# A decoder trunk in split float32: two of three products joined in one 512-column matmul

## The chip, the cores and the metric

The kernel runs on one core of a Trainium2 chip. The metric is the device time of the core in microseconds (us), from runs of the whole program. The engines are TensorE (PE; its weight loads are shown apart as PEld), VectorE (DVE), ScalarE (ACT), GpSimd (POOL) and SyncE (SP), which issues the DMAs. Weights come from HBM; SBUF is the on-chip memory with 128 partitions; PSUM takes the results of TensorE in eight banks, each 128 partitions by 512 float32 values.

## The reference

The input is x with 256 tokens of 1024 values. The program is two layers. Each is wrapped by two half-step SwiGLU FFNs, so there are four FFNs, called a, b, c and d here. Between a and b stands a chunked gMLP (u, v, a spatial mixing of v), between c and d a stick-breaking attention, whose shared keys and values are computed between b and c.

```python
def swiglu(h, w_in, w_out):              # w_in 1024 x 5632, w_out 2816 x 1024
    gate, up = jnp.split(h @ w_in, 2, axis=-1)
    return (jax.nn.silu(gate) * up) @ w_out

x = x + 0.5 * swiglu(rms_norm(x, g), w_in, w_out)     # four of these

z = jax.nn.gelu(h @ a_w_in)              # gMLP, a_w_in 1024 x 4096
u, v = jnp.split(z, 2, axis=-1)
x = x + (u * (W_s @ layer_norm(v) + b)) @ a_w_out
```

All values are float32.

## The kernel before

**Products.** The weights are streamed as pieces of 128 x 1024 in the order of use: a DMA into `raw` (7 buffers), a ScalarE cast to the high part `whi` (L81, 9 buffers), a VectorE subtraction to the low part `wlo` (L83, 9 buffers). x is split in the same way into `xnh` and `xnl`. A product of full precision is three matmuls that add up in PSUM (`mm3`, L148 to L150): low weights by high x, high weights by low x, high weights by high x, each over 256 tokens, that is 256 columns.

**An FFN.** Its 2816 features are 11 blocks of 256. `ffn_in(j)` makes block j of gate and up: two matrices, 8 chunks of 128 along the contraction, 2 halves of 128 features, so 32 triples. Gate and up have one PSUM bank each, the two halves side by side. Then VectorE multiplies each bank by `rb`, the 1/rms of each token (L449 gate, L451 up), ScalarE takes silu of gate (L450), VectorE multiplies the two (L452), and the result is split into `hh` (ScalarE, L153) and `hl` (VectorE, L154). The output block `out(j)`, 16 triples, multiplies these by two pieces of the second matrix into the four `y` banks. The order is in(0), in(1), then out(j) and in(j+2) by turns; at the end the rest of out(9) and out(10) goes block by block of x (`close`), and each x block is scaled, split again and squared at once. In FFN d the output products stand the other way round, with 512 columns (`yo`), and transposes of x (`xb`, L809) lie behind in(1).

**PSUM.** Two pools of four banks each, taken in rotation: `gbank` for input blocks and everything that is used briefly, `ybank` for the residual stream. A bank is taken again as soon as the last reader of its old contents is done.

**Other users of gbank in FFN a.** Behind out(3) and out(4) the spatial weights are transposed (`pws`, read by one VectorE copy each), behind out(5) and out(6) `spatial_bias` makes a row sum in one bank (`prs`, L516), which eight VectorE instructions read (L519).

**u.** `u_in` makes 256 features of u in one bank by 16 triples, eight times; one multiplication by `rb` (L585) and a gelu follow.

**Order.** Every engine runs its queue in order. A recording layer orders the instructions of each engine by priorities and dependencies, so the place of the casts of later weight pieces between an FFN's own instructions is not that of the program text. Each cast of a piece waits until the piece nine places earlier in the stream has had its last product.

Of the kernel before, what the change touches and what calls it, by code (L numbers as in the profile page):

```python
# [28 lines left out]
WARM = 6, 10  # L29
# The attention's order of issue, by blocks of two heads: q (four heads' queries), z (scores), p  # L30
# (weights), t (weights transposed), v (values), o (products into the residual stream, in the
# banks that y sets up).
ATT_STEPS = (
# [5 lines left out]
class Weights:  # L39
    """The weight matrices as a stream of [128, 1024] pieces in the order of use. Each is loaded  # L40
    once and split exactly into two float32r parts, w = hi + lo, some pieces ahead of its use."""

    def __init__(self, tc, raw_pool, hi_pool, lo_pool):
        self.nc = tc.nc
        self.keep_order = tc.keep_in_program_order
        self.strict = False
        self.behind = 0  # so many pieces keep their place
        self.piece = UNIT
        self.pools = raw_pool, hi_pool, lo_pool
        self.sources = []  # L50
        self.raw = {}
        self.parts = {}
        self.loaded = 0
        self.split = 0
# [5 lines left out]
    def order(self, ins):  # L60
        """Keeps an instruction behind those traced ahead of it, where the order matters."""
        return self.keep_order(ins) if self.strict else ins
# [37 lines left out]
def trunk(  # L100
# [44 lines left out]
    def mm3(o, a, b, first, last):  # L145
        """o (+)= a.T @ b for a, b each given as two float32r parts."""
        (ah, al), (bh, bl) = a, b
        nc.tensor.matmul(o, al, bh, start=first, stop=False, skip_group_check=True)  # L148
        nc.tensor.matmul(o, ah, bl, start=False, stop=False, skip_group_check=True)  # L149
        nc.tensor.matmul(o, ah, bh, start=False, stop=last, skip_group_check=True)  # L150
# [4 lines left out]

    # The gMLP's blocks of 256 features: the u products, the mixing behind them, the products into
    # the residual stream behind that.
    U_STEPS = [("in", 0), ("in", 1)]
# [5 lines left out]

# [1 line left out]
    W = Weights(tc, rawp, hip, lop)  # L166
# [7 lines left out]
    def plan_in_out(n, ins, w_out):  # L174
        """Pairs of blocks: columns of the first matrix, then, one pair later, the rows that they
        meet in the second."""
        steps = {}
        for j in range(n + 1):
            if j < n:
                steps["in", j] = [[W.add(cols(w, c0 + 256 * j, kh)) for w, c0 in ins] for kh in range(2)]  # L180
            if j:
                steps["out", j - 1] = [W.add(rows(w_out, 256 * (j - 1) + P * m)) for m in range(2)]
        return steps
# [19 lines left out]

# [1 line left out]
    xin = {}  # L205
# [37 lines left out]
    def warm_up(n):  # L243
        """Products of nothing, that wake the tensor engine's clock while the first loads run."""
        bank = gbank("warm")
        for _ in range(n):
            W.order(nc.tensor.matmul(bank[:, :P], ones, ones, start=True, stop=True))
# [11 lines left out]

# [1 line left out]
    xT = act.tile([P, KC, T], F32, name="xT")  # L261
    xnh = act.tile([P, KC, T], F32R, name="xnh")
    xnl = act.tile([P, KC, T], F32R, name="xnl")
    acc = act.tile([P, T], F32, name="acc")
# [4 lines left out]
    def prepare(d, gains, sq=True):  # L269
        """The parts of x*g of chunk d for the next products, and its share of the mean square."""  # L270
        for (name, i), h, l in gains:
            g = gain(name, i * KC + d)
            W.order(nc.scalar.activation(h[:, d, :], xT[:, d, :], AF.Copy, scale=g))
            W.order(
                nc.vector.scalar_tensor_tensor(
                    l[:, d, :], xT[:, d, :], g, h[:, d, :].bitcast(F32), ALU.mult, ALU.subtract
                )
            )
        if sq:
            square(d)  # L280
# [12 lines left out]
    def newton(o, root, v, w):  # L293
        """o = v**-0.5 from an estimate of v**0.5, with a step of Newton's; w is scratch."""
        nc.vector.reciprocal(o, root)
# [4 lines left out]
    class Rms:  # L300
        """1/rms of each token: first as a column per 128 tokens (rT), then along the free axis on
        all partitions (rb)."""

# [23 lines left out]

# [1 line left out]
    def load_x(hf):  # L329
        """Half of x into the residual stream, its parts and its squares."""  # L330
        for d in range(hf * 4, hf * 4 + 4):
# [32 lines left out]
    def bc2(ap):  # L364
        """[128, n] -> [128, 2, n], the same twice."""
        return ap.unsqueeze(1).broadcast_to([P, 2, ap.shape[1]])

    def pair(ap):
        return ap.rearrange("p (m t) -> p m t", m=2)

# [1 line left out]
    class Residual:  # L372
        """y.T = sum over chunks of W[chunk].T @ h[chunk], in four banks."""

# [12 lines left out]
    def close(y, tail, head, scale, gains):  # L387
        """The last chunks block by block, so that each block of x is ready early; head blocks of
        the first of them go ahead."""
        w, h = tail[0]  # L390
# [10 lines left out]
    def project(outs, ids, xs, mid={}, by_bank=False):  # L401
        """outs += W.T x for blocks of 256 features: [features, tokens] of two halves each. mid:
        what else is done behind a number of groups."""
        groups = []
# [3 lines left out]
        for n, group in enumerate(groups):  # L408
# [12 lines left out]
            if n + 1 in mid:  # L421
                mid[n + 1]()

    def project_rows(o, ids, xs, mid={}):
        """x.T W for a block of 256 features: [tokens, features] of two halves."""
        for kh in range(2):
# [16 lines left out]
    def ffn_in(tag, j, ids, mid={}, by_bank=False):  # L443
        """silu(gate) * up of 256 features, in two parts."""
        banks = [gbank(f"g{tag}_{j}"), gbank(f"u{tag}_{j}")]
        project(banks, ids, XN, mid, by_bank)
        gs = scratch(f"gs{tag}_{j}")
        us = scratch(f"us{tag}_{j}")
        nc.vector.tensor_mul(pair(gs), pair(banks[0]), bc2(rb))  # L449
        nc.scalar.activation(gs, gs, AF.Silu)  # L450
        nc.vector.tensor_mul(pair(us), pair(banks[1]), bc2(rb))  # L451
        nc.vector.tensor_mul(us, us, gs)  # L452
# [8 lines left out]
    def ffn(tag, plan, gains, mid={}, by_bank=False, extra={}):  # L461
        """extra: what else is done ahead of a block's products into the residual stream."""
        hs = {0: ffn_in(tag, 0, plan["in", 0], mid, by_bank), 1: ffn_in(tag, 1, plan["in", 1])}
# [13 lines left out]

    # ======== layer 0: gMLP ========
    sgu = ExitStack()
# [16 lines left out]
    def spatial_weights(hf):  # L496
        """The causal W_s, transposed, and what the LayerNorm's shift and b_s add behind it:
        b_c * (row sum of W_s)[t] + b_s[t]."""
        gg = slice(hf * 4, hf * 4 + 4)
# [44 lines left out]

    # v, tokens on partitions; its LayerNorm without gain and shift, which come behind W_s.
    vsb = sg.tile([P, 2, DA], F32, tag="vsb", name="vsb")
# [34 lines left out]
    def u_in(j):  # L581
        bank = gbank(f"uu{j}")
        project([bank], [[i] for i in plan_u["in", j]], XN)
        u = sg.tile([P, 512], F32, tag="u", name=f"usb{j}", bufs=4)
        nc.vector.tensor_mul(pair(u), pair(bank), bc2(rb))  # L585
        nc.scalar.activation(u, u, AF.Gelu_apprx_tanh)
        return u
# [47 lines left out]

    # ======== shared K and V, and layer 1: stick-breaking attention ========
    att = ExitStack()
# [10 lines left out]

    # k, transposed; the row half of each head is its own, the other half is zero.
    XK = (xkh, xkl)  # L650
# [7 lines left out]
    for r in range(2):  # L658
# [3 lines left out]
        for t in kz:  # L662
            nc.gpsimd.dma_start(t[oo, r::2, 1 - r, :].bitcast(F32), t[rr, r::2, r, :].bitcast(F32))
    # v, tokens on partitions, each head twice.
    vf = scratch("vf")
# [25 lines left out]
    def weights_of(b, q):  # L691
        """A of heads 2b and 2b+1: sigmoid(z) times the product of sigmoid(-z) over the keys
        between; [queries, heads, keys] for each block of queries."""
        kv = b // 2
# [102 lines left out]

    # ======== the last FFN, its output with tokens on partitions, and the final norm ========
    fin = ctx.enter_context(tc.tile_pool(name="fin", bufs=1))
# [102 lines left out]
```

## Time and profile before

| | us |
|---|---|
| median of 3 runs | 1019.38 (1019.08 to 1020.25) |
| profiled execution, its span | 1016.9 |
| busy in the span: TensorE | 998.7 (98%) |
| weight loads | 979.4 (96%) |
| VectorE | 651.4 (64%) |
| ScalarE | 499.6 (49%) |
| GpSimd | 84.0 (8%) |

The span runs from the first to the last instruction that the profiler saw in one execution; no time of that execution other than its span is given, and the runs' median lies 2.5 us above the span. Busy is the sum of the instructions' own times; matmuls are pipelined and their ends modelled, so a product's cost is read from the distance between two starts. The granted clock of TensorE stood in the topmost tenth in all of the 40 slices of the span.

### The profile page before, as it was taken

To read this page: it belongs to the slowest core of one execution; us is meant where nothing else is said; L and a number is where in the kernel's file an instruction comes from. 1 tells how busy PE (TensorE), PEld (TensorE's weight loads), DVE (VectorE), ACT (ScalarE), POOL (GpSimd) and SP (SyncE) were. 2 spreads that over 40 slices of the span, in tenths; PEclk is the share of its full clock that TensorE was granted. 3 is DMA by queue.
4 is the path that set the end of the run, shared out by engine and by line. 5 is a ranking of instruction groups with operands and counts; after the bars stand their busy time and mean duration, and the time that the engine had idled before them with its cause. 6 is when DMAs were issued, how large, how long until landed. Compare 5 with 4: busy or idle time off the path is not lost.

```text
span 1016.9 us, 19320 instructions
## 1 busy us (share of the span) xinstructions
PE 998.7 (98%) x8044; PEld 979.4 (96%) x8044; DVE 651.4 (64%) x852; ACT 499.6 (49%) x683; POOL 84.0 (8%) x122
## 2 busy tenths in 40 slices
PE   9999999999999999999999999999998899999997
PEld 8999999999999999999999999999998799999996
DVE  6865665676766774646569655564679975655553
ACT  7543434475544553434348444443476565444433
POOL 3000000010000300000003000000036420000002
PEclk9999999999999999999999999999999999999999
DMA  9965555656545365655564756555642436656511
GB/s 310 325 187 174 185 179 176 187 161 212 186 167 167 125 214 183 187 184 187 180 190 141 239 185 187 182 188 181 193 132 65 137 117 219 188 185 191 183 42 42
DMA packets 135208, 179.56 MB, mean 177 GB/s; under 512 B 5624, under 2 KB 119376, under 8 KB 135120
## 3 DMA queue, kind: packets, MB, share of 16 engines
q1 hardware_dynamic: 134768, 177.76, 54.9%
q8 instruction: 63, 1.03, 0.4%
q0 software_dynamic: 192, 0.52, 0.2%
q14 instruction: 25, 0.20, 0.1%
q10 hardware_dynamic: 160, 0.05, 0.0%
HBM read 176.73 MB, written 1.05 MB: 175 GB/s over the span
## 4 chain that ended last, share of the span: by engine, by line
PE 88%; DVE 6%; issue 2%; ACT 1%; DMA 1%; POOL 1%; SPq 0%; ACTq 0%; POOLq 0%; DVEq 0%
PE yo L148 2%; PE yo L150 2%; PE yo L149 2%; PE gb L148 2%; PE uc L149 2%; PE gc L148 2%; PE ub L149 2%; PE yb L148 2%; PE uc L150 2%; PE ub L150 2%; PE ub L148 2%; PE gb L150 2%; PE uc L148 2%; PE ud L150 2%; PE gc L150 2%
## 5 line engine op out<-in xcount | busy, mean ns | idle before, releaser
L81 ACT CAST whi<-raw 128x1024 fp32r<-128x1024 f32 (+1 forms) x333 | 342.3, 1044 | 403.3 <-issue 219.2
L83 DVE TENSOR_TENSOR wlo<-raw,whi 128x1024 fp32r<-128x1024 f32 (+1 forms) x333 | 400.9, 1221 | 203.2 <-ACT whi L81 202.4
L288 POOL TENSOR_TENSOR acc<-acc,sq 128x256 f32<-128x256 f32 x39 | 33.9, 870 | 566.9 <-ACT sq L287 564.9
L148 PE MATMUL ga<-xnh,wlo 128*128 128x256 f32 x176 | 50.7, 288 | 0.0
L148 PE MATMUL ya<-hha,wlo 128*128 128x256 f32 x176 | 50.0, 284 | 0.1
L148 PE MATMUL yc<-hhc,wlo 128*128 128x256 f32 x176 | 50.0, 284 | 0.1
L148 PE MATMUL yb<-hhb,wlo 128*128 128x256 f32 x176 | 50.0, 284 | 0.0
L148 PE MATMUL gd<-xnh,wlo 128*128 128x256 f32 x176 | 50.0, 284 | 0.0
L148 PE MATMUL gb<-xnh,wlo 128*128 128x256 f32 x176 | 49.9, 283 | 0.0
L148 PE MATMUL gc<-xnh,wlo 128*128 128x256 f32 x176 | 49.9, 283 | 0.0
L149 PE MATMUL ya<-hla,whi 128*128 128x256 f32 x176 | 49.8, 283 | 0.0
L149 PE MATMUL yb<-hlb,whi 128*128 128x256 f32 x176 | 49.8, 283 | 0.0
L149 PE MATMUL yc<-hlc,whi 128*128 128x256 f32 x176 | 49.7, 283 | 0.0
L150 PE MATMUL ud<-xnh,whi 128*128 128x256 f32 x176 | 49.7, 282 | 0.0
L150 PE MATMUL uc<-xnh,whi 128*128 128x256 f32 x176 | 49.6, 282 | 0.0
L149 PE MATMUL ub<-xnl,whi 128*128 128x256 f32 x176 | 49.6, 282 | 0.0
L149 PE MATMUL uc<-xnl,whi 128*128 128x256 f32 x176 | 49.6, 282 | 0.0
L150 PE MATMUL yb<-hhb,whi 128*128 128x256 f32 x176 | 49.6, 283 | 0.0
L148 PE MATMUL ua<-xnh,wlo 128*128 128x256 f32 x176 | 49.6, 282 | 0.0
L150 PE MATMUL ga<-xnh,whi 128*128 128x256 f32 x176 | 49.6, 282 | 0.0
L150 PE MATMUL ub<-xnh,whi 128*128 128x256 f32 x176 | 49.6, 282 | 0.0
L149 PE MATMUL gd<-xnl,whi 128*128 128x256 f32 x176 | 49.5, 281 | 0.0
(286 smaller groups left out, 3367.1 us busy)
## 6 DMA issues: line engine op xcount, KB each, us to landing
raw<-in_ffn_w_in_dram SPq DMA_DIRECT2D x176, 512.0 KB, 4.6
raw<-in_ffn_w_out_dram SPq DMA_DIRECT2D x88, 512.0 KB, 4.2
raw<-in_a_w_in_dram SPq DMA_DIRECT2D x32, 512.0 KB, 4.4
raw<-in_a_w_out_dram SPq DMA_DIRECT2D x16, 512.0 KB, 3.3
raw<-in_b_w_q_dram SPq DMA_DIRECT2D x8, 512.0 KB, 4.4
raw<-in_b_w_o_dram SPq DMA_DIRECT2D x8, 512.0 KB, 4.3
raw<-in_w_kv_dram SPq DMA_DIRECT2D x4, 512.0 KB, 4.2
xin<-in_x_dram SPq DMA_DIRECT2D x4, 256.0 KB, 4.5
```

The source lines that it names most:

```text
L81: ins = nc.scalar.copy(hi[:, cc], raw[:, cc])
L83: ins = nc.vector.tensor_sub(lo[:, cc], raw[:, cc], hi[:, cc].bitcast(F32))
L148: nc.tensor.matmul(o, al, bh, start=first, stop=False, skip_group_check=True)
L149: nc.tensor.matmul(o, ah, bl, start=False, stop=False, skip_group_check=True)
L150: nc.tensor.matmul(o, ah, bh, start=False, stop=last, skip_group_check=True)
L288: nc.gpsimd.tensor_add(acc, acc, s)
```

## The change

`xnh` and `xnl` become two halves of one tile `xnb` of [128, 2, 8, 256], so that chunk k of both can be given to one matmul as 512 columns. A new `project_wide` takes the place of `project` in `ffn_in` and `u_in`: for each chunk and half of the features, low weights by high x go into the first 256 columns of a bank, and high weights by both parts of x into all 512 columns. The right 256 columns thus hold the addend from the low part of x, and a bank holds one half of 128 features, not two. `ffn_in` takes four banks in place of two, `u_in` two in place of one. A new `gather` reads them: for each bank a ScalarE copy of the right half to SBUF, a VectorE addition of the left half and that copy; then one VectorE multiplication by `rb` over both. All other products (output blocks, v, K and V, attention) keep `mm3`. The diff also removes comments and docstrings.

```diff
-    xnh = act.tile([P, KC, T], F32R, name="xnh")
-    xnl = act.tile([P, KC, T], F32R, name="xnl")
+    xnb = act.tile([P, 2, KC, T], F32R, name="xnb")
+    xnh = xnb[:, 0]
+    xnl = xnb[:, 1]
...
+    def project_wide(outs, ids, mid={}, by_bank=False):
+        groups = []
+        for kh in range(2):
+            group = [(kh, b, i) for b, i in zip(outs, ids[kh])]
+            groups += [[g] for g in group] if by_bank else [group]
+        for n, group in enumerate(groups):
+            ws = [(kh, b, W.get(i, 256)) for kh, b, i in group]
+            for k4 in range(4):
+                for kh, b, w in ws:
+                    k = kh * 4 + k4
+                    for m in range(2):
+                        wh, wl = (t[:, k4, m * P : (m + 1) * P] for t in w)
+                        nc.tensor.matmul(
+                            b[m][:, :T], wl, xnh[:, k, :], start=k == 0, stop=False, skip_group_check=True
+                        )
+                        nc.tensor.matmul(
+                            b[m], wh, xnb[:, :, k, :], start=False, stop=k == KC - 1, skip_group_check=True
+                        )
+            if n + 1 in mid:
+                mid[n + 1]()
+
+    def gather(o, banks, name):
+        for m, bank in enumerate(banks):
+            mm = slice(m * T, (m + 1) * T)
+            r = scratch(f"{name}_{m}", T)
+            nc.scalar.copy(r, bank[:, T:])
+            nc.vector.tensor_add(o[:, mm], bank[:, :T], r)
+        nc.vector.tensor_mul(pair(o), pair(o), bc2(rb))
...
     def ffn_in(tag, j, ids, mid={}, by_bank=False):
-        banks = [gbank(f"g{tag}_{j}"), gbank(f"u{tag}_{j}")]
-        project(banks, ids, XN, mid, by_bank)
+        banks = [[gbank(f"{n}{tag}_{j}_{m}") for m in range(2)] for n in "gu"]
+        project_wide(banks, ids, mid, by_bank)
         gs = scratch(f"gs{tag}_{j}")
         us = scratch(f"us{tag}_{j}")
-        nc.vector.tensor_mul(pair(gs), pair(banks[0]), bc2(rb))
+        gather(gs, banks[0], f"gr{tag}_{j}")
         nc.scalar.activation(gs, gs, AF.Silu)
-        nc.vector.tensor_mul(pair(us), pair(banks[1]), bc2(rb))
+        gather(us, banks[1], f"ur{tag}_{j}")
         nc.vector.tensor_mul(us, us, gs)
...
     def u_in(j):
-        bank = gbank(f"uu{j}")
-        project([bank], [[i] for i in plan_u["in", j]], XN)
+        banks = [gbank(f"uu{j}_{m}") for m in range(2)]
+        project_wide([banks], [[i] for i in plan_u["in", j]])
         u = sg.tile([P, 512], F32, tag="u", name=f"usb{j}", bufs=4)
-        nc.vector.tensor_mul(pair(u), pair(bank), bc2(rb))
+        gather(u, banks, f"uur{j}")
         nc.scalar.activation(u, u, AF.Gelu_apprx_tanh)
```

The order of the instructions changes at three places that the prediction speaks of. The first is TensorE's queue in FFN b's block 5, one chunk of the contraction (`gb_5` and `ub_5` are the banks of gate and up, with a half's number at the end in the new kernel). Before, where the second half's three rows read like the first's and are left out:

```order
L148 MATMUL gb_5_5099<-xnh_116,wlo142_4918 128x256
L149 MATMUL gb_5_5099<-xnl_117,whi142_4917 128x256
L150 MATMUL gb_5_5099<-xnh_116,whi142_4917 128x256
...
L148 MATMUL ub_5_5100<-xnh_116,wlo143_4972 128x256
L149 MATMUL ub_5_5100<-xnl_117,whi143_4971 128x256
L150 MATMUL ub_5_5100<-xnh_116,whi143_4971 128x256
```

Now:

```order
L440 MATMUL gb_5_0_4738<-xnb_116,wlo142_4577 128x256
L443 MATMUL gb_5_0_4738<-xnb_116,whi142_4576 128x512
L440 MATMUL gb_5_1_4739<-xnb_116,wlo142_4577 128x256
L443 MATMUL gb_5_1_4739<-xnb_116,whi142_4576 128x512
L440 MATMUL ub_5_0_4740<-xnb_116,wlo143_4615 128x256
L443 MATMUL ub_5_0_4740<-xnb_116,whi143_4614 128x512
L440 MATMUL ub_5_1_4741<-xnb_116,wlo143_4615 128x256
L443 MATMUL ub_5_1_4741<-xnb_116,whi143_4614 128x512
```

Twelve instructions of 256 columns became four of 256 and four of 512, into four banks.

The second place is ScalarE's queue at the end of FFN c, behind its last input block, 10 (`gsc`, `usc`: gate and up in SBUF; `grc`, `urc`: the copies of the right halves). Before:

```order
L81 CAST whi253_8541<-raw253_8527 128x1024
L450 ACTIVATE gsc_10_8517<-gsc_10_8517 128x512
L81 CAST whi254_8547<-raw254_8533 128x1024
L153 CAST hhc_10_8523<-usc_10_8518 128x512
L81 CAST whi255_8700<-raw255_8539 128x1024
```

Now:

```order
L454 COPY grc_10_0_7840<-gc_10_0_7746 128x256
L81 CAST whi253_7874<-raw253_7860 128x1024
L454 COPY grc_10_1_7843<-gc_10_1_7747 128x256
L454 COPY urc_10_0_7848<-uc_10_0_7748 128x256
L81 CAST whi254_7880<-raw254_7866 128x1024
L454 COPY urc_10_1_7851<-uc_10_1_7749 128x256
L81 CAST whi255_8033<-raw255_7872 128x1024
L484 ACTIVATE gsc_10_7838<-gsc_10_7838 128x512
L153 CAST hhc_10_7856<-usc_10_7839 128x512
```

Four copies stand ahead of the silu, with three casts of weights between them; before, one cast stood ahead of it. The cast of piece 255 moved from behind `hhc_10` to ahead of the silu.

The third is VectorE's queue in FFN a, behind input block 6, where `prs0` is the bank of the first `spatial_bias`. Before:

```order
L83 TENSOR_TENSOR wlo45_1590<-raw45_1515,whi45_1589 128x1024
L452 TENSOR_TENSOR usa_6_1506<-usa_6_1506,gsa_6_1505 128x512
L83 TENSOR_TENSOR wlo46_1596<-raw46_1545,whi46_1595 128x1024
L154 TENSOR_TENSOR hla_6_1512<-usa_6_1506,hha_6_1511 128x512
L83 TENSOR_TENSOR wlo47_1650<-raw47_1587,whi47_1649 128x1024
L519 SCALAR_TENSOR_TENSOR bias_193<-prs0_1575,gT1_102,wsbs_194 128x128 x8
L83 TENSOR_TENSOR wlo48_1656<-raw48_1593,whi48_1655 128x1024
```

Now:

```order
L83 TENSOR_TENSOR wlo46_1471<-raw46_1418,whi46_1470 128x1024
L456 TENSOR_TENSOR usa_6_1367<-usa_6_1367,rb_118 128x512
L83 TENSOR_TENSOR wlo47_1509<-raw47_1462,whi47_1508 128x1024
L486 TENSOR_TENSOR usa_6_1367<-usa_6_1367,gsa_6_1366 128x512
L553 SCALAR_TENSOR_TENSOR bias_192<-prs0_1448,gT1_102,wsbs_193 128x128 x3
L154 TENSOR_TENSOR hla_6_1385<-usa_6_1367,hha_6_1384 128x512
L553 SCALAR_TENSOR_TENSOR bias_192<-prs0_1448,gT1_102,wsbs_193 128x128 x5
L83 TENSOR_TENSOR wlo48_1515<-raw48_1468,whi48_1514 128x1024
```

The low part of block 6, `hla_6`, moved into the middle of the eight reads of `prs0`; these were in one run ahead of the split of piece 48 before.

## Rows read from the trace of the kernel before

**Rows 1.** The page: span, and busy time of each engine.
```profile
span 1016.9 us, 19320 instructions
...
PE 998.7 (98%) x8044; PEld 979.4 (96%) x8044; DVE 651.4 (64%) x852; ACT 499.6 (49%) x683; POOL 84.0 (8%) x122
```

**Rows 2.** The page: chain that ended last, by engine.
```profile
PE 88%; DVE 6%; issue 2%; ACT 1%; DMA 1%; POOL 1%; SPq 0%; ACTq 0%; POOLq 0%; DVEq 0%
```

**Rows 3.** Timeline of PE, FFN c (start us, busy us, engine line op out<-in).
```profile
580.59 0.28 PE L148 MATMUL gc<-xnh,wlo 128*128 128x256 f32 x1
...
591.95 0.28 PE L148 MATMUL yc<-hhc,wlo 128*128 128x256 f32 x1
...
597.69 0.28 PE L148 MATMUL gc<-xnh,wlo 128*128 128x256 f32 x1
```

**Rows 4.** Timeline of PE, FFN d, an output block of 512-column products.
```profile
964.39 0.40 PE L148 MATMUL yo<-whi,hld 128*128 128x512 f32 x1
...
969.65 0.39 PE L150 MATMUL yo<-whi,hhd 128*128 128x512 f32 x1
...
969.88 0.28 PE L148 MATMUL gd<-xnh,wlo 128*128 128x256 f32 x1
```

**Rows 5.** Windows, an input and an output block (busy us and count, PEclk, DMA, GB/s).
```profile
580.60:592.00 11.40, 11.40 (x99) 11.40 (x98) 4.08 (x4) 3.57 (x4) 0.00 (x0) 1.00 0.66 203
592.00:597.70 5.70, 5.70 (x50) 5.70 (x50) 5.49 (x7) 3.57 (x5) 0.00 (x0) 1.00 0.45 155
```

**Rows 6.** Groups by form, VectorE (line, operation, shapes, count; busy us, mean ns; idle before).
```profile
L83 DVE TENSOR_TENSOR wlo<-raw,whi 128x1024 fp32r<-128x1024 f32 x331 | 399.6, 1224 | 203.2 <-ACT whi L81 202.4
...
L449 DVE TENSOR_TENSOR gsc<-gc,rb 128x512 f32<-128x512 f32 x11 | 7.6, 691 | 23.1 <-PE gc L150 23.1
...
L396 DVE SCALAR_TENSOR_TENSOR xT<-yc,xT 128x256 f32<-128x256 f32 x8 | 3.3, 418 | 0.6 <-PE yc L150 0.4
```

**Rows 7.** Groups by form, ScalarE.
```profile
L81 ACT CAST whi<-raw 128x1024 fp32r<-128x1024 f32 x331 | 341.1, 1046 | 403.3 <-issue 219.2 <-PE gb L150 43.7 <-PE ga L150 38.2
...
L153 ACT CAST hhc<-usc 128x512 fp32r<-128x512 f32 x11 | 6.8, 621 | 6.2 <-DVE usc L452 6.2
...
L325 ACT COPY rb<-pstf 128x256 f32<-128x256 f32 x3 | 1.1, 361 | 0.0
```

**Rows 8.** Timeline of VectorE, end of FFN c.
```profile
729.61 1.21 DVE L83 TENSOR_TENSOR wlo<-raw,whi 128x1024 fp32r<-128x1024 f32 x1
730.74 0.69 DVE L452 TENSOR_TENSOR usc<-usc,gsc 128x512 f32<-128x512 f32 x1
```

**Rows 9.** Timeline of ScalarE, end of FFN c.
```profile
728.33 1.05 ACT L81 CAST whi<-raw 128x1024 fp32r<-128x1024 f32 x1 [3.68 <-issue]
...
731.46 0.62 ACT L153 CAST hhc<-usc 128x512 fp32r<-128x512 f32 x1 [0.61 <-DVE usc L452]
...
731.99 1.04 ACT L81 CAST whi<-raw 128x1024 fp32r<-128x1024 f32 x1
```

**Rows 10.** Timeline of PE: FFN a block 7, FFN c's end, FFN d's transposes.
```profile
128.07 1.02 PE L516 MATMUL prs<-wsT,ones 128*128 128x512 f32 x2
...
128.52 0.68 PE L148 MATMUL ga<-xnh,wlo 128*128 128x256 f32 x1
...
728.80 0.28 PE L148 MATMUL yc<-hhc,wlo 128*128 128x256 f32 x1
...
731.55 0.28 PE L150 MATMUL yc<-hhc,whi 128*128 128x256 f32 x1
...
733.83 0.28 PE L148 MATMUL yc<-hhc,wlo 128*128 128x256 f32 x1
...
844.71 1.91 PE L809 MATMUL xb<-ident,xT 128*128 128x128 f32 x16
...
846.38 0.48 PE L148 MATMUL yo<-whi,hld 128*128 128x512 f32 x1
```

**Rows 11.** Timeline of VectorE, FFN a: spatial_bias.
```profile
129.13 2.16 DVE L519 SCALAR_TENSOR_TENSOR bias<-prs,gT,wsbs 128x128 f32<-128x128 f32 x8 [1.31 <-PE prs L516]
```

## The prediction

> **What bounds the kernel now.** I read the page's line of busy times first [rows 1]: TensorE is busy 998.7 of 1016.9 us, VectorE 64%, ScalarE 49%. The chain that ended last is TensorE for 88% and VectorE for 6% [rows 2]. So nearly every microsecond of TensorE's queue counts, and work on the other two engines counts only where TensorE waits for it. A busy PE is not PE at its peak, so the timeline of PE came next, in stretches without a break. From 580.59 to 591.95 us stand 96 products of 256 columns: 11.36/96 = 118.3 ns from start to start; 591.95 to 597.69 gives 48 at 119.6 [rows 3]. From 964.39 to 969.88 stand 24 products of 512 columns: 228.7 ns each [rows 4]. The granted clock there is 1.00, the upper level of 2.4 GHz [rows 5]. A product of 512 columns thus costs 1.93 of one of 256, not 1.
>
> The table by windows shows where slack is missing [rows 5]. Over an input block with the output block behind it (17.1 us) VectorE is busy 9.58 us, but 5.49 of these lie in the 5.70 us behind the input block. The queue that empties the banks is full exactly there.
>
> **What the products give.** A triple of 256 columns is replaced by one of 256 and one of 512. Four FFNs of 11 blocks with 2 x 8 x 2 triples are 1408, the u part 8 x 16 = 128, together 1536. Each goes from 3 x 118.3 = 354.9 ns to 118.3 + 228.7 = 347.0: 7.9 ns x 1536 = 12.1 us gained. No row shows the two widths in alternation. If the short product takes half of the long one, 114.4, the gain is 11.8 x 1536 = 18.1 us; if the long one costs two short ones, nothing. I take 12.1, the rows as they are.
>
> The Trainium skill (TensorE: Matmul & The Clock Gate, "Back-to-back issue gap") gives a sustained 131 ns for a 512-column product. By that the triple would cost 118.3 + 131 = 249 ns and the change save some 162 us (an estimate); the row, 228.7 ns, says otherwise and decides.
>
> **What the evacuation costs in work.** A pair of banks was read by one multiplication from PSUM, 0.691 us [rows 6]. Now two ScalarE copies read it (nearest row 0.361, 256 columns from PSUM, [rows 7]) and two VectorE additions of 256 columns (nearest row 0.418, [rows 6]); the multiplication stays, from SBUF (0.69, as the product at 730.74, [rows 8]). For 96 pairs that is some 69 us more on ScalarE and 80 on VectorE. Both stay far under TensorE's total, so the sum does not matter; the places do.
>
> **What the evacuation costs in waits.** An input block now fills all four banks of its pool. Whoever next needs a bank there waits until its addition has run. Call them g0, g1 (gate) and u0, u1 (up). Let t = 0 be TensorE's first slot behind an input block. The last k-step's products end, by the spacings above and a 512-column product's 0.39 us [rows 4], at -0.88 (gate's first bank), -0.53, -0.19 and +0.16 (up's second). I let both queues run in the new order, with the rows' durations [rows 6, 7], each instruction starting about 0.08 us ahead of the end before it on its engine (729.61 + 1.21 = 730.82 against a start at 730.74, [rows 8]) and 0.03 us behind another engine's (730.74 + 0.69 = 731.43 against 731.46, [rows 8, 9]):
> ScalarE: copy g0 -0.83 to -0.46; cast of weights -0.45 to 0.60; copy g1 0.51 to 0.87; copy u0 0.80 to 1.16; cast 1.08 to 2.13; copy u1 2.04 to 2.40.
> VectorE: add g0 -0.43 to -0.02; split of weights 0.63 to 1.85; add g1 1.77 to 2.18; add u0 to 2.52; gate times rb to 3.12; add u1 3.04 to 3.46; split 3.38 to 4.60; up times rb 4.52 to 5.20; split to 6.34; product us*gs 6.26 to 6.94.
> So the four banks are free at 0.0, 2.2, 2.5 and 3.5. Whose turn is next?
>
> - An output block of 5.7 us lies behind (36 of the input blocks): the next input wants up's second bank at +6.7, and 3.2 us of slack remain. Nothing is lost.
> - FFN's blocks 0 and 1 stand back to back. Block 1 wants the banks at 0.0, 0.35, 0.69 and 1.04 behind its start. With 0.24 us of the norm's rows between them and the rb copy (0.361, [rows 7]) in ScalarE's queue, second bank and fourth cost 1.1 and 0.9: 2.0 us in FFN b. d has the same queue: 2.0. c has a split more in it: 2.5. In a, whose loading of x and norm put more there, I take 3.5. Sum 10.0.
> - In d the transposes of x back, 1.91 us before [rows 10], stand behind block 1 and use the same pool; they are now laced with output products, and the second group wants at 1.55 (a quarter of 844.71 to 846.38 and five products of 0.229) what is free at 2.2: 0.65, and with the last one, whose bank is free at 3.5, I take 1.0.
> - spatial_bias: the row of ones' products takes one bank behind out(5) (0.45 us, 128.07 to 128.52, [rows 10]), its eight reads on VectorE take 2.16 us [rows 11]. Before, the pool's next user of that bank came an input block later; now it is the fourth bank of the input block right behind, wanted at 5.74 + 0.45 + 1.04 = 7.2. Between the third and the fourth read stands hl of block 6, which waits for its ScalarE half; that stands behind a cast that waits for out(5)'s last product (5.9 to 7.0), so it ends at 7.6, hl follows at 8.3, five reads of 0.27 end at 9.7. Loss 2.5, twice: 5.0.
> - spatial_weights: a copy of 512 columns (0.691) ends at 7.55 behind us*gs where the bank is wanted near 7.1; with a hand-over to TensorE some 0.55, twice: 1.1.
> - The FFN's end: block 10 in FFN a, b and c has no input block behind it but its own consumer. Before, the first product with hh of block 10 stood at 733.83, 5.0 us behind the input block's end at 728.80, and us*gs was done at 731.43 [rows 8, 10]. Now us*gs ends at 6.94, since two splits, four adds and the later silu come ahead of it; the silu stands behind a cast that waits for the 24th output product (731.55 before, cast at 731.99, [rows 9, 10]), here 3.03. hh (0.621) is ready at 7.6. A hand-over between TensorE and another engine took 0.16 (731.55 + 0.28 = 731.83 against 731.99). The new order puts 45 products ahead of hh, 45 x 0.1196 = 5.4: 7.6 + 0.1 - 5.4 = 2.3 lost, and 0.1 on hl, three times 2.4 = 7.2. In d eleven more products of 512 columns go ahead: nothing.
> - u blocks 2 and 3: 0.3. K, V and attention: the banks come free earlier than they are wanted.
>
> Sum of the waits 10.0 + 1.0 + 5.0 + 1.1 + 7.2 + 0.3 = 24.6 us. Net: 24.6 - 12.1 = 12.5 slower. On the profiled execution's span that is 1016.9 + 12.5 = 1029.4; the runs' median lies 2.5 above that span (1019.38 - 1016.9), so 1031.9.
>
> **Rivals.**
> A. The short product beside a long one costs its columns only: gain 18.1, 1019.4 + 24.6 - 18.1 = 1025.9. For it: 228.7/2 = 114.4 [rows 4]. Against: the step from 512 back to 256 took 0.23, and 256-column products alone take 118.3 [rows 3, 4].
> B. (faster) The casts of weights do not stand in the way, because they run earlier than my queue has them; then every bank is free about when its own copy and add are done. Blocks 0 and 1: 0.5 + 0.5 + 0.7 + 1.1; spatial_bias 2 x 1.3; the ends none: 5.4 us. 1019.4 + 5.4 - 12.1 = 1012.7. It turns to faster below 12.1 us of waits. For it: before, ScalarE idled 3.68 us ahead of the cast at 728.33 [rows 9], so its queue had room. Against: casts of the pieces that the block itself used can't run before its products end (731.99 right behind 731.55, [rows 9, 10]).
> C. The steady blocks wait too: if a copy or an add takes over twice its row or the casts fall behind, up's bank is free only after +6.7. At 1 us for each of 36 blocks: 1031.9 + 36 = 1068. It decides from 3.2 us of extra delay on. Against: 5.49 us of VectorE's work there grows by 1.7 and runs over into an input block where it is busy 4.08 of 11.4 [rows 5]. The Trainium skill (Perfetto Trace Analysis, "Optimizing Tensor Performance") wants matmul groups to rotate through banks so that one is emptied under the next; with all four taken at once only the output block covers that, and no row yet shows whether it does.
> D. The weights' loading paces TensorE (PEld 96%, [rows 1]) and a product costs the same at any width: 1536 x 118.3 = 182 us less, 1019.4 - 181.7 + 24.6 = 862. Against: 512-column products, one load each, came every 228.7 ns [rows 4].
>
> **How the numbers follow.** Forecast 0.65 (1025 to 1038), A 0.12 (1021 to 1029), B 0.11 (1008 to 1019), C 0.09 (1038 to 1070), D 0.03. What can be told from no change here is some 0.2%, 2 us. Forecast, A and C are slower; B is mostly faster, and its upper part with A's and the forecast's lower edges gives the cases within 0.2%. Faster 0.14, same 0.08, slower 0.78. The range 1018 to 1041 leaves out most of B, of C, and D.
>
> **What would show it.** Start-to-start: 118 and 229 ns in alternation, an input block of 11.1 us instead of 11.36. Gaps in PE of 1 to 2 us behind block 0 of each FFN, of 2.3 ahead of the first hh of block 10, of 2.5 in FFN a's blocks 7 and 8, each released by an add or hh on VectorE; none at the other input blocks. TensorE's busy share should fall from 98% to about 95%. The forecast is wrong if these gaps sum to under 12 us, if gaps repeat behind every output block, or if the pair of products does not cost 347 ns.

## The result, and the profile after

Four runs took 1029.88 us in the median (1028.99 to 1031.52), against 1019.44 for the kernel before: a ratio of 1.0100, interval 1.0088 to 1.0113. The change makes the kernel 10.4 us slower; 1031.9 was forecast. The profiled execution took 1028.99 us with a span of 1027.3, 10.4 more than the span before. The total was nearly right, but not by the terms of the sum: the gain and the waits were both put too high, and the two errors met.

The page of the changed kernel, its span, busy times and chain:

```profile
span 1027.3 us, 16737 instructions
...
PE 999.8 (97%) x6508; PEld 906.5 (88%) x6508; DVE 716.8 (70%) x1044; ACT 558.7 (54%) x875; POOL 84.7 (8%) x122
...
PE 86%; DVE 9%; issue 2%; ACT 1%; DMA 1%; POOL 0%; SPq 0%; ACTq 0%; DVEq 0%; POOLq 0%
```

Beside [rows 1, 2]: the chain's VectorE share rose from 6% to 9%, and weight loads fell from 96% to 88% without a gain in time. VectorE's busy time grew by 65 us and ScalarE's by 59, somewhat less than the 80 and 69 that were worked out.

The timeline of PE in a steady input block of FFN c (start us, busy us):

```profile
588.28 0.28 PE L440 MATMUL gc<-xnb,wlo 128*128 128x256 f32 x1
...
590.04 0.28 PE L440 MATMUL gc<-xnb,wlo 128*128 128x256 f32 x1
590.16 0.39 PE L443 MATMUL gc<-xnb,whi 128*128 128x512 f32 x1
590.39 0.28 PE L440 MATMUL uc<-xnb,wlo 128*128 128x256 f32 x1
590.51 0.40 PE L443 MATMUL uc<-xnb,whi 128*128 128x512 f32 x1
590.75 0.28 PE L440 MATMUL uc<-xnb,wlo 128*128 128x256 f32 x1
...
599.58 0.28 PE L148 MATMUL yc<-hhc,wlo 128*128 128x256 f32 x1
```

From 588.28 to 599.58 are 11.30 us for 32 pairs, 353.1 ns a pair; before, a triple took 355.0 [rows 3]. The 512-column products cost 229 and 240 ns by turns, 234.5 on average, not the 228.7 of [rows 4].

That price does occur in the same kernel, though. The first three blocks of u, the same kind of products in the same alternation:

```profile
254.12 0.28 PE L440 MATMUL uu<-xnb,wlo 128*128 128x256 f32 x1
...
270.77 0.60 PE L629 MATMUL mix<-wsT,vsb 128*128 128x128 f32 x4
```

These are 16.65 us for 48 pairs, 346.9 ns a pair, with 512-column products of 229.1 on average. In FFN c's block 0 they took 229 or 230 as well.

The windows of that block and the output block behind it, in the columns of [rows 5]:

```profile
588.30:599.60 11.30, 11.30 (x67) 9.82 (x66) 5.71 (x7) 4.40 (x6) 0.00 (x0) 1.00 0.70 206
599.60:605.30 5.70, 5.70 (x49) 5.70 (x48) 5.15 (x9) 3.86 (x7) 0.00 (x0) 1.00 0.42 146
```

TensorE is busy without a break in both, so here the gathering is hidden. VectorE does 10.86 us in 17.0, and the extra work has run over into the input block (5.71 where 4.08 stood).

The waits of PE, longest first (what it waited for, us in total, times, longest); rows that stand in the kernel before as well are left out:

```profile
PE ya L148 <- ACT hha L153: 2.1, 1, 2.1
PE yb L148 <- ACT hhb L153: 2.1, 1, 2.1
PE yc L148 <- ACT hhc L153: 2.1, 1, 2.1
...
PE kT L149 <- DVE xkl L276: 0.9, 1, 0.9
...
PE ga L443 <- DVE xnb L276: 0.6, 1, 0.6
PE ua L440 <- DVE wlo L83: 0.5, 1, 0.5
...
PE gc L440 <- DVE gsc L455: 0.2, 1, 0.2
```

None is released by a bank at a block's start for more than 0.2 us (the last row). The three ends of FFNs are where it waits. Here is VectorE at the end of FFN c (block 10 ends on TensorE at 736.00):

```profile
736.62 1.23 DVE L83 TENSOR_TENSOR wlo<-raw,whi 128x1024 fp32r<-128x1024 f32 x1 [0.59 <-ACT whi L81]
737.76 0.42 DVE L455 TENSOR_TENSOR gsc<-gc,grc 128x256 f32<-128x256 f32 x1
738.10 0.41 DVE L455 TENSOR_TENSOR usc<-uc,urc 128x256 f32<-128x256 f32 x1
738.43 0.68 DVE L456 TENSOR_TENSOR gsc<-gsc,rb 128x512 f32<-128x512 f32 x1
739.03 0.42 DVE L455 TENSOR_TENSOR usc<-uc,urc 128x256 f32<-128x256 f32 x1
739.36 1.22 DVE L83 TENSOR_TENSOR wlo<-raw,whi 128x1024 fp32r<-128x1024 f32 x1
740.50 0.68 DVE L456 TENSOR_TENSOR usc<-usc,rb 128x512 f32<-128x512 f32 x1
741.10 1.22 DVE L83 TENSOR_TENSOR wlo<-raw,whi 128x1024 fp32r<-128x1024 f32 x1
742.23 0.68 DVE L486 TENSOR_TENSOR usc<-usc,gsc 128x512 f32<-128x512 f32 x1
```

ScalarE and TensorE there:

```profile
742.95 0.62 ACT L153 CAST hhc<-usc 128x512 fp32r<-128x512 f32 x1 [2.29 <-DVE usc L486]
```

```profile
741.28 0.28 PE L150 MATMUL yc<-hhc,whi 128*128 128x256 f32 x1
743.62 0.62 PE L148 MATMUL yc<-hhc,wlo 128*128 128x256 f32 x3 [2.06 <-ACT hhc L153]
```

From 736.62 to 742.91 VectorE has no gap. The product us*gs ends 6.91 us behind block 10 (6.94 forecast), where before it ended 2.63 behind it [rows 8, 10]. ScalarE's hh ends at 7.57 (7.6 forecast), and TensorE, out of other products at 741.40, waits.

Where the 10.3 us between the profiled spans (10.4 by the rounded figures) arose, from the starts of the first products of each stretch:

| stretch | before | after | difference |
|---|---|---|---|
| start to FFN a's out(0) | 35.5 | 37.1 | +1.6 |
| FFN a, out(0) to out(8) | 139.9 | 139.5 | -0.3 |
| FFN a's end, to the gMLP's norm | 34.8 | 37.4 | +2.6 |
| v and u | 137.3 | 136.9 | -0.5 |
| FFN b, in(0) to out(8) | 162.6 | 162.0 | -0.6 |
| FFN b's end, K and V | 41.8 | 46.4 | +4.6 |
| FFN c, in(0) to out(8) | 159.8 | 159.6 | -0.2 |
| FFN c's end, to the attention's norm | 34.9 | 37.3 | +2.4 |
| attention | 73.5 | 73.6 | +0.1 |
| FFN d, to the last product | 189.5 | 189.0 | -0.5 |
| behind the last product | 7.4 | 8.4 | +1.0 |

FFN b's end costs 2 us more than the other two. Windows of the changed kernel there (PEclk is the last but two):

```profile
535.00:537.50 2.50, 0.54 (x5) 0.34 (x3) 1.91 (x3) 0.56 (x1) 0.00 (x0) 1.00 0.68 199
537.50:538.40 0.90, 0.79 (x5) 0.60 (x5) 0.69 (x1) 0.06 (x1) 0.00 (x0) 0.93 0.94 148
538.40:541.60 3.20, 3.20 (x15) 3.20 (x16) 1.15 (x3) 1.33 (x4) 0.00 (x0) 0.50 0.33 131
```

TensorE was idle for 2 us; 0.7 us after it began again the granted clock fell to 0.50, the 1.2 GHz level, for over 3 us. Fifteen products took 213 ns each in the third window, not 119: 1.4 us. Then K waits 0.9 us for a part of x (the kT row above).

### The profile page after: what moved, and what is told of

Its sections match the earlier page's. It is cut to its first block, busy times and chain, and to the rows that moved or that the text cites. A ratio compares the mean times of both kernels' runs of the same rounds, so it can differ in the third digit from the quotient of the medians.

```text
span 1027.3 us, 16737 instructions
## 1 busy us (share of the span) xinstructions
PE 999.8 (97%) x6508; PEld 906.5 (88%) x6508; DVE 716.8 (70%) x1044; ACT 558.7 (54%) x875; POOL 84.7 (8%) x122
## 4 chain that ended last, share of the span: by engine, by line
PE 86%; DVE 9%; issue 2%; ACT 1%; DMA 1%; POOL 0%; SPq 0%; ACTq 0%; DVEq 0%; POOLq 0%
PE gb L443 4%; PE ub L443 4%; PE ud L443 4%; PE gd L443 4%; PE ga L443 4%; PE gc L443 4%; PE uc L443 4%; PE ua L443 4%; PE uu L443 3%; PE yo L148 2%; PE yo L149 2%; PE yo L150 2%; PE gb L440 2%; PE ub L440 2%; PE ud L440 2%; PE gd L440 2%
## 5 line engine op out<-in xcount | busy, mean ns | idle before, releaser
L443 PE MATMUL ga<-xnb,whi 128*128 128x512 f32 x176 | 66.5, 398 | 0.6 <-DVE xnb L276 0.6
L443 PE MATMUL ub<-xnb,whi 128*128 128x512 f32 x176 | 66.2, 397 | 0.0
L443 PE MATMUL ud<-xnb,whi 128*128 128x512 f32 x176 | 66.2, 397 | 0.0
L443 PE MATMUL gb<-xnb,whi 128*128 128x512 f32 x176 | 66.1, 396 | 0.0
L443 PE MATMUL gd<-xnb,whi 128*128 128x512 f32 x176 | 66.1, 397 | 0.0
L443 PE MATMUL uc<-xnb,whi 128*128 128x512 f32 x176 | 66.1, 397 | 0.0
L443 PE MATMUL gc<-xnb,whi 128*128 128x512 f32 x176 | 66.0, 396 | 0.0
L443 PE MATMUL ua<-xnb,whi 128*128 128x512 f32 x176 | 65.9, 397 | 0.0
L440 PE MATMUL ga<-xnb,wlo 128*128 128x256 f32 x176 | 50.9, 289 | 0.0
L440 PE MATMUL gc<-xnb,wlo 128*128 128x256 f32 x176 | 49.9, 284 | 0.2 <-DVE gsc L455 0.2
```

Source lines behind the costliest of these rows:

```text
L440: nc.tensor.matmul(b[m][:, :T], wl, xnh[:, k, :], start=k == 0, stop=False, skip_group_check=True)
L443: nc.tensor.matmul(b[m], wh, xnb[:, :, k, :], start=False, stop=k == KC - 1, skip_group_check=True)
```

## The experiments

Ratios are to the kernel before, in runs on the same chip. Theory W: the time is lost in reading the banks, nearly all of it at the FFNs' ends, and joining gives about 3 us. Its rivals: F, joining gives the forecast's 12.1 us and more waits hide it; N, the reading is not what costs.

**1. No gathering** (e1_left_half).

```diff
-            r = scratch(f"{name}_{m}", T)
-            nc.scalar.copy(r, bank[:, T:])
-            nc.vector.tensor_add(o[:, mm], bank[:, :T], r)
-        nc.vector.tensor_mul(pair(o), pair(o), bc2(rb))
+            nc.vector.tensor_mul(o[:, mm], bank[:, :T], rb)
```

> The joined products as in the changed kernel, in four banks, but the banks are read without the gathering: VectorE multiplies the left half of each bank by rb, and nothing is copied or added (so the low part of x is left out of gate, up and u). Theory W (the loss is in the way the banks are read, and the products gave 2.6 us in all, 0.06 us per input block): no waits at the ends of FFN a, b and c, input blocks of 11.30 us, time 1014 to 1018 us. Rival F (the products gave the 12.1 us of the forecast, and waits of 22 us hide it): 1006 to 1009 us. Rival N (the reading is not what costs): 1027 to 1031 us.

1025.0 us, 1.0051 (1.0036 to 1.0066): none of the three. The waits at the ends are gone and the blocks take 11.30 us, as W has it, but new waits stand behind block 0 of a, b and d. PE's waits:

```profile
PE ga L440 <- DVE gsa L453: 2.0, 1, 2.0
PE gb L440 <- DVE gsb L453: 1.7, 1, 1.7
PE gd L440 <- DVE gsd L453: 1.7, 1, 1.7
```

The multiplication that now empties the banks needs rb, which is made at just that point; the additions of the changed kernel do not. F is out. That the ends' waits come from the gathering is shown; the experiment put another wait in their place.

**2. The two parts of x side by side** (e2_adjacent).

```diff
-    xnb = act.tile([P, 2, KC, T], F32R, name="xnb")
+    xnb = act.tile([P, KC, 2, T], F32R, name="xnb")
```

> Only the layout of x is changed: the two parts of a chunk lie side by side, so that the 512 columns are one run of memory instead of two. A 512-column product took 234.5 us/1000 between two of 256, and 228.7 ns among its like. Theory L (the two separate runs cost the 6 ns): 512-column products at 228.7 ns, input blocks of 11.1 us, 9 us less than the changed kernel, 1020 to 1022 us. Theory A (the change of width costs them): blocks stay at 11.30 us and the time within 1 us of the changed kernel's.

1028.87 us, 1.0094 (1.0077 to 1.0110), blocks of 11.30 us: the layout is not what makes the 512-column products dear.

**3. Ordered by width** (e3_by_width): for each chunk the four low-weight products, then the four wide ones.

```diff
             for k4 in range(4):
-                for kh, b, w in ws:
+                for wide in range(2):
+                  for kh, b, w in ws:
```

> Only the order of the products is changed: for each chunk of the contraction first the four of 256 columns, then the four of 512, so that the width changes twice in eight products and not eight times. Theory A (the change of width costs 6 ns each): input blocks near 11.15 us, 6 to 9 us less than the changed kernel, 1021 to 1024 us, if the banks, which are now wanted within 0.5 us of each other, are free. Theory L (layout): blocks stay at 11.30 us, 1029 to 1031 us.

1028.36 us, 1.0080 (1.0065 to 1.0095). Blocks take 11.23 us, half of what A wanted, and the time lies above A's window: 350.9 ns a pair, so wide products at some 232.6 ns. The waits at the ends grew from 2.1 to 2.4 us.

**4. Block 10 as before the change** (e4_last_narrow).

```diff
+        if j == NPAIR - 1:
+            banks = [gbank(f"g{tag}_{j}"), gbank(f"u{tag}_{j}")]
+            project(banks, ids, XN, mid, by_bank)
```

> Block 10 of each FFN alone is computed as before (three products of 256 columns, two banks, no gathering); all else as in the changed kernel. Theory W: the waits of 2.2 us for hh at the ends of FFN a, b and c go, and with them what followed the one in b (the lower clock for 3 us, about 1.6 us, and a wait of 1.05 us for a part of x in K): 8 to 10 us less, 1020 to 1022 us. Rival: the waits only move to the next reader, since VectorE and ScalarE have the casts to do all the same: 1026 to 1030 us.

1018.26 us, 0.9985 (0.9976 to 0.9994): 1.1% less than the changed kernel, a little below the expected window. No wait at any FFN's end is left, the granted clock stays up there, and K does not wait. With 40 of the 44 input blocks and u still joined, the kernel is faster than before. W holds, N is out.

**5. Gathering without joining** (e5_narrow_gather).

```diff
-                            b[m], wh, xnb[:, :, k, :], start=False, stop=k == KC - 1, skip_group_check=True
+                            b[m][:, T:], wh, xnl[:, k, :], start=False, stop=False, skip_group_check=True
+                        )
+                        nc.tensor.matmul(
+                            b[m][:, :T], wh, xnh[:, k, :], start=False, stop=k == KC - 1, skip_group_check=True
```

> Reading of the banks as in the changed kernel, but no joined product: the low-x product goes into the right half of the bank and the high-x product into the left half as two matmuls of 256 columns each. The difference to the changed kernel is what joining alone saves. Theory M (measured spacing, 1.9 ns per triple): input blocks of 11.36 us, 2 to 4 us slower than the changed kernel, 1031 to 1035 us. Rival F (the forecast's 7.9 ns per triple): 12 us slower, 1041 to 1043 us.

1033.24 us, 1.0142 (1.0129 to 1.0156), 0.4% above the changed kernel; blocks of 11.36 us. Joining alone is worth 3 to 4 us, not 12.

**6 and 7. Block 10 as before, with order by width** over one chunk (e6_width_narrow, experiments 3 and 4 together) or over half of the contraction (e7_half_narrow).

```diff
-            for k4 in range(4):
-                for wide in range(2):
+            for wide in range(2):
+                for k4 in range(4):
```

> Block 10 as before the change, the other blocks with the products of a chunk ordered by width (four of 256 columns, then four of 512). Theory: the two effects add, 40 blocks of 11.23 instead of 11.30 us take 2.8 us off the 1018.3 of block 10 alone: 1015 to 1017 us, faster than both kernels. Rival: the four banks are now wanted within 0.5 us of each other, and the waits behind block 0 of each FFN (0.5 us in FFN c when only the order was changed) give it back: 1017.5 to 1019.5 us.

> As the kernel before in this list, but ordered by width over half of the contraction: 16 products of 256 columns, then 16 of 512. Theory A2 (a 512-column product takes 231 to 236 ns in the first eight behind a change of width and 226.5 from then on, as in FFN d's output block): input blocks near 11.14 us, 1012 to 1014.5 us. Rival (the 512-column products of these blocks stay at 231 ns however long the run is): blocks near 11.2 us, 1015 to 1017 us, more if the low parts of the weights, now wanted first, come late.

1015.39 us, 0.9969 (0.9958 to 0.9980), and 1015.74 us, 0.9972 (0.9961 to 0.9984); blocks of 11.23 and 11.25 us. The two effects add. A run of 16 wide products is no cheaper than one of four, so A2 fell.

**8. Gathering done twice, block 10 as before** (e8_twice).

```diff
+            r2 = scratch(f"{name}_{m}x", T)
+            nc.scalar.copy(r2, bank[:, T:])
+            nc.vector.tensor_add(o[:, mm], bank[:, :T], r2)
```

> Block 10 as before the change, and in all other blocks and in u each copy and each addition of the gathering is done twice (the second overwrites the first). Theory S (an output block behind an input block leaves 3.2 us of slack, so what the reading costs there is hidden): 1018 to 1020.5 us, within 2 us of the 1018.3 with single reading. Rival C (the steady blocks are near their limit): a wait behind each output block, 0.5 to 1 us for 36 blocks, 1034 us or more.

1032.67 us, 1.0136 (1.0122 to 1.0150): a miss for S as a sum, and yet the blocks behind an output block still take 11.30 us, so they do have the slack. Nearly all was lost where input blocks stand back to back, which the expectation had left out (some 1 us in u; in FFN d the granted clock fell behind the wait, too):

```profile
PE gb L440 <- DVE gsb L458: 2.2, 1, 2.2
PE gd L440 <- DVE gsd L458: 2.2, 1, 2.2
PE gc L440 <- DVE gsc L458: 2.2, 1, 2.2
```

**9. TensorE's order held** (e9_kept_order).

```diff
-                        nc.tensor.matmul(
+                        keep(nc.tensor.matmul(
...
+            project_wide(banks, ids, mid, by_bank, tc.keep_in_program_order if j in (1, 7, 8) else lambda ins: ins)
```

> Block 10 as before the change; and in the input blocks 1 of FFN a, b and c, and 7 and 8 of FFN a, whose banks are still being read when they begin, TensorE's products are held in the order of the program text (both halves of gate, both of up, chunk by chunk). (d's block 1 too.) Without that, the recorded order runs up to nine products of the first bank ahead. Theory R (this rearrangement on TensorE is what made the forecast waits vanish): waits of about 1.8 us behind block 0 of each FFN and 2.4 us in each of a's blocks 7 and 8, together 12 us more than the 1018.3 of block 10 alone (0.9985 of the kernel before), so 1.009 to 1.012 of the kernel before. Rival: the banks came free early enough anyway: within 3 us of 0.9985, at most 1.002.

1030.09 us, 1.0114 (1.0093 to 1.0134), as R has it. FFN b's block 1 took 13.21 us against 11.45 with the free order, d's 13.34 against 11.60. From FFN a's out(0) to out(8) 3.1 us more than in experiment 4 were lost, where R had 4.8; 2.2 of them are one wait for `hha`, not for a bank. PE at the start of b's block 1 with the order held:

```profile
368.17 0.47 PE L440 MATMUL gb<-xnb,wlo 128*128 128x256 f32 x1
368.47 0.39 PE L443 MATMUL gb<-xnb,whi 128*128 128x512 f32 x1
369.54 0.39 PE L440 MATMUL gb<-xnb,wlo 128*128 128x256 f32 x1 [0.68 <-DVE gsb L455]
...
371.02 0.39 PE L440 MATMUL ub<-xnb,wlo 128*128 128x256 f32 x1 [0.52 <-DVE usb L455]
```

The changed kernel itself there:

```profile
365.06 0.47 PE L440 MATMUL gb<-xnb,wlo 128*128 128x256 f32 x1
365.36 0.39 PE L443 MATMUL gb<-xnb,whi 128*128 128x512 f32 x1
365.59 0.28 PE L440 MATMUL gb<-xnb,wlo 128*128 128x256 f32 x1
365.71 0.40 PE L443 MATMUL gb<-xnb,whi 128*128 128x512 f32 x1
365.95 0.28 PE L440 MATMUL gb<-xnb,wlo 128*128 128x256 f32 x1
```

It works on in gate's first bank: nine products of that bank stand ahead of the first of gate's second.

**10. All products wide** (e10_all_wide, one run).

```diff
-                            b[m][:, :T], wl, xnh[:, k, :], start=k == 0, stop=False, skip_group_check=True
+                            b[m], wl, xnb[:, :, k, :], start=k == 0, stop=False, skip_group_check=True
```

> The low weights meet both parts of x as well, so that all products of the input blocks and of u have 512 columns (one term more is computed than in the other kernels). It measures what a 512-column product of this kind costs among its like. Theory A (the change of width is what makes it dear): 226 to 229 ns from start to start, input blocks of 14.5 to 14.7 us. Theory O (it is the operands: these products take 231 to 235 ns in any company): 14.8 to 15.1 us.

1198.25 us. Blocks of 14.93 us, 64 products at 233.3 ns: O's window. Among their like, too, these products cost more than FFN d's output products. That the operands are the reason, as O says, does not follow: the first blocks of u in the changed kernel have operands of the same kinds, at 229.1.

**11 and 12. One bank after the other** (e11_bank_major), and by width within a bank (e12_bank_width), all input blocks joined.

```diff
-            for k4 in range(4):
-                for kh, b, w in ws:
-                    k = kh * 4 + k4
-                    for m in range(2):
+            for kh, b, w in ws:
+                for m in range(2):
+                    for k4 in range(4):
+                        k = kh * 4 + k4
```

> All input blocks joined as in the changed kernel, block 10 too; only the order of the products differs: for each half of the contraction, all four chunks of one bank, then the next bank (gate's two, then up's two). Gate's banks are then complete 2.8 us and 1.4 us earlier than up's second, and their copies and additions run while TensorE still works on up. Theory T (the waits at the ends of FFN a, b and c come from four copies and four additions queued behind the block's last product): us*gs is done about 3.5 us behind block 10, the first product with hh comes at 5.0 us, no wait; with blocks of 11.30 us 1016 to 1019 us. Theory B (the 512-column products were dear because each went to another bank than the one before): blocks near 11.1 us, 1009 to 1013 us. Rival: the casts of weights stand in the queue all the same and the waits stay over 1 us each: 1023 us or more.

> As the kernel before in this list, and within a bank the four products of 256 columns first, then the four of 512. Theory: no waits at the ends as there, and 0.07 us less per input block as when the order by width was tried alone (44 blocks, 3.1 us, a little more than with block 10 left out): 1014 to 1016 us, the fastest of all, 0.995 to 0.997 of the kernel before. Rival: the order by width helped only because four banks took turns: blocks of 11.30 us, the same time as the kernel before in this list.

1018.25 us, 0.9995 (0.9986 to 1.0004), with blocks of 11.30 us and no wait for hh at the ends (K's wait of 0.9 us for a part of x stays): T, not B. And 1014.89 us, 0.9955 (0.9941 to 0.9969), with blocks of 11.23 us: the fastest of all, 4.1 us under the kernel before. VectorE and ScalarE at the end of FFN c in the latter, whose block 10 ends at 726.21:

```profile
723.08 0.42 DVE L457 TENSOR_TENSOR gsc<-gc,grc 128x256 f32<-128x256 f32 x1
724.06 0.42 DVE L457 TENSOR_TENSOR gsc<-gc,grc 128x256 f32<-128x256 f32 x1 [0.56 <-ACT grc L456]
...
726.87 0.42 DVE L457 TENSOR_TENSOR usc<-uc,urc 128x256 f32<-128x256 f32 x1 [0.18 <-ACT urc L456]
...
729.08 0.69 DVE L488 TENSOR_TENSOR usc<-usc,gsc 128x512 f32<-128x512 f32 x1
```

```profile
730.23 0.62 ACT L153 CAST hhc<-usc 128x512 fp32r<-128x512 f32 x1
```

Gate's additions lie ahead of the block's end, us*gs ends 3.56 us behind it (3.5 expected), and hh at 730.85 is in time for the product 42 places on, 5.0 us behind the end.

## Why the prediction was right, and where it was not

- **What bounds the kernel.** Right: VectorE's 65 us and ScalarE's 59 us of added work cost time only at the three places where TensorE had nothing else to do.
- **The products.** This term was mis-sized. 7.9 ns a triple were taken from [rows 3, 4] for all 1536 triples; 1.9 were measured in the steady blocks (11.36 to 11.30 us a block), so 44 x 0.06 in the FFNs and 0.4 in u give 3 us, not 12.1. The failing step is the 228.7 ns taken as the price of every wide product. Some stretches do have it, and with it the pair at 347 ns: u's first three blocks and FFN c's block 0, in experiment 2 blocks 5 and 6 of FFN a, in experiment 11 blocks 0 and 1 of FFN c. In most blocks a wide product takes 232 to 235 ns on average, in every order (experiments 3, 7, 10) and layout (2). Why a stretch has the one price or the other is open. Rival A leaned the other way and is out (the short product took 118.8 beside the long one), as is D.
- **The steady blocks.** Right: no wait behind an output block, even with the gathering doubled. Rival C is out.
- **Blocks 0 and 1, the transposes in d, spatial_bias and spatial_weights.** Wrong: 17.1 us were forecast, and no wait of a bank over 0.2 us was found. The times at which VectorE frees the banks were about right (the fourth at 367.85, 2.8 us behind block 1's start in FFN b); the step that failed is "block 1 wants the banks at 0.0, 0.35, 0.69 and 1.04". TensorE's own queue had been rearranged around the late banks. The order of the changed kernel says so, and it was read there for ScalarE and VectorE but for TensorE only at the ends and at d's transposes. Experiment 9 takes the rearrangement away in blocks 1, 7 and 8 and loses some 12 us; for d's transposes and `spatial_weights` (2.1 of the 17.1) it was not tried.
- **The ends of FFN a, b and c.** Right in mechanism and size: 2.4 each were forecast, 2.1 waited, 2.6 and 2.4 lost in a and c. In b 4.6 were lost: the fall of the clock and K's wait for x were not foreseen. K's wait does not hang on hh alone: it stays in experiments 11 and 12.
- **Rival B** (faster) is out: the casts do stand in the queue, and with a gain of 3 us it would have needed waits of under 3.
- **Not in the sum.** 1.0 us behind the last product: the reciprocal root of the first 128 tokens ended later on VectorE. The runs tie it to block 10: where that is gathered from four banks in turn, this stretch takes 8.4 us (experiments 2 and 5) or 9.2 (3); where it is narrow, not gathered or joined bank by bank, 7.4 (1, 4, 6, 7, 9, 11, 12; 7.9 in 8). 1.6 us ahead of FFN a's out(0): the kernels 2 and 4, with the same products there, needed 35.8 and 36.0, so most of it need not come with the change. In this execution a cast of weights waited 1.8 us for its DMA there, 0.6 and 0.8 in those two and 0.9 in the kernel before.

Against the forecast's +12.5 us, the gain was 9 us too high and the waits some 17 us, and about 5 us came from what no term foresaw (2.3 in FFN b's end, 1.0 at the end, up to 1.6 at the start): 9 - 17 + 5 = -3, where -2.2 was found. The agreement of the total was luck and proves none of the terms. Two of the prediction's own signs of being wrong came about: the gaps that it named sum to 6.3 us, under 12, and the pair cost 353 ns in most blocks, not 347.

## What to carry to other kernels

When a change fills every bank of a pool, look for the block whose consumer is next instead of another block: there the emptying is bare, and finishing one bank after the other (experiment 11) removes the wait without giving up the change. Read the new order of every engine on which a wait is forecast, the waiting one above all: a scheduler may have put other work into the gap. Take a matmul's price from more than one stretch (the same products stood at 229 and at 234.5 ns in one execution), and check the terms of a sum against the trace even when its total is right.

## What the runs showed of the hardware

- A 512-column product of float32r took 223 to 237 ns in FFN d's output blocks and 229 to 240 in the joined blocks, against 118.3 on average for 256 columns. The sustained 131 ns of the Trainium skill (TensorE: Matmul & The Clock Gate, "Back-to-back issue gap") is shown by no run here. What makes the difference between 229 and 234.5 is open. Operands, order and layout are the same at both prices, and run length and change of width leave 232 to 235 on average. The other engines' work does not explain it: in FFN d's last block, where all of them and the DMA are idle, the wide products took 234.4 on average.

```profile
999.00:1006.00 7.00, 7.00 (x42) 6.07 (x41) 0.00 (x0) 0.00 (x0) 0.00 (x0) 1.00 0.00 0
```

- An idle TensorE of about 2 us was followed in some executions by a granted clock of 0.50 for some 3 us, in others not, for the same wait: in the changed kernel's profile at the end of FFN b but not of a and c, in experiment 2 at a, in experiment 3 at b and c. In experiments 1, 2, 5, 6, 10 and 12 it also fell in the attention, behind a wait of 1.7 us that the kernel before has too; its profile shows no fall there. Four runs of the changed kernel had mean clocks of 0.996, 0.994, 0.993 and 0.991 and took 1028.99, 1029.09, 1030.67 and 1031.52 us. What decides it is open.
